# Bias rows at the gate projection, and attention by pairs of heads, in a one-core fp32 two-block kernel

## The chip, the cores and the metric

The kernel runs on one core of a Trainium2 chip. The metric is the device time of one execution in microseconds (us). A profiled execution gives, besides its time, a trace of every instruction and transfer; its span (first to last instruction) is a little shorter than its time.

## What is computed

Two transformer blocks in a row on x of 1 x 256 x 1024, all in fp32. The first has a hybrid mixer (a gated delta rule in chunks of 64, and a short convolution, joined by two sigmoid gates) and a SwiGLU FFN, both with adaptive norm. The second has causal attention with a relative bias by distance, 16 heads of 64, and a gated FFN with a convolution. With 256 positions the block selection of the attention leaves one block, so only the part of the query's own block counts:

```python
    s_own = jnp.einsum('bhqd,bhkd->bhqk', qi, k_own) * scale
    s_own = s_own + rel_bias[:, rel_bucket(qpos[:, None] - kpos_own[None, :])]
    s_own = jnp.where(kpos_own[None, :] <= qpos[:, None], s_own, NEG)
    ...
    p = jax.nn.softmax(jnp.concatenate(logits, axis=-1), axis=-1)
    out = jnp.einsum('bhqk,bhkd->bhqd', p[..., kk * BS:], v_own)
    ...
x = first_block(x, ...)          # mixer: w_in, gated delta rule, w_gdn_proj, w_o; FFN: w_ffn_in, w_ffn_out
y = rms_norm_2(h, attn_norm); qkv = y @ w_qkv; h = h + attention @ w_o_2
h = h + (silu(gate) * val) @ w_down   # gate, val = conv(rms_norm_2(h) @ w_up)
```

## The kernel before

All activations stay on the chip, feature-major (128 features of a tile on the partitions, 256 positions along the row). A weight comes in chunks of 1 MB (`raw`, four buffers), whose DMAs are issued on SP (lines 327 to 349). ACT copies a chunk's upper part (`whi`, rounded to the fast matmul format), and DVE or POOL makes the rest, `wlo = raw - whi` (`emit_event`, from line 368; `pool_free`, line 98, decides whether POOL gets a half chunk, 128x512, or DVE a full one, 128x1024). Every product is then three matmuls: `whi` by the high part of the activation, `whi` by its low part, `wlo` by the high part (the last loop of the quoted code). A unit is 128 output columns of one weight over all its rows.

The order of the instructions on each engine is set when the program is built. The main loop goes through the units in a fixed order and issues their matmuls; after each `k` it calls `tick`, which advances generators, one per piece of other work (`start(...)` puts one on the list): the delta rule's inversions and steps, the norms, the attention's heads. A generator's `yield` lets other work go first. How far each is advanced depends on a model of the engines' times, `et`, which `account` (line 111) keeps: it adds a cost for each instruction issued, and for a DMA one by its size, from the line that the change touches (line 118). All instructions are issued through one helper, so all have line 150 in the profile, and are told apart by the names of their tiles: `mm` and `sd` are PSUM tiles (main products and side products), `h1h`/`h1l`, `o`, `mixh`, `h2nh`, `ah`, `xah`, `oath` are activations in two parts, in the order of the stages: w_in (to about 340 us; its last piece is the projection of gate A), w_gdn_proj, w_o, FFN in, FFN out (from about 510 us), then w_qkv with the attention between its units (615 to 695), w_o_2, w_up, w_down.

The relative bias is kept as a table by distance. `rel_table` (line 1291) is started when the FFN's out projection begins (`rel_at`). It loads a one-hot matrix, multiplies the 16 x 32 bias by it (16 heads x 256 distances), writes the result behind NEG into `relr`, 16 partitions x 384, and sends that to DRAM 128 times per head in one DMA (`relscr`, 3,072 KB). Two gathers of 1 MB, `relb`, then read it with a row step of 383 instead of 384, so each partition gets the row shifted by one. These DMAs are on POOL's queue, as are the powers of the delta rule's output norm (`osc`).

The attention runs by heads. `att_probs(j, e)` makes the scores of head e of tile j (two heads of 64 share a tile of 128 features; each lies on one half of the partitions, so its matmuls use 64 rows): query positions 0 to 127 against keys 0 to 127, positions 128 to 255 against all keys. DVE adds the bias and takes the maximum, ACT exponentiates and sums, PE transposes three 128x128 blocks (`oats` into `oatp`). `att_out(j)` transposes the values, scales them, multiplies with the transposed probabilities as weights (six matmuls 128x64 a tile, three for each head), divides by the sums on DVE (`gx<-sd,rcp`), transposes the result back (two transposes of `gx`) and splits it into `oath` and `oatl`.

Of the kernel before, what the change touches and what calls it, by code (L numbers as in the profile page):

```python
# [11 lines left out]
F32 = mybir.dt.float32  # L12
F32R = mybir.dt.float32r
AF = mybir.ActivationFunctionType
# [58 lines left out]
def body(ctx, tc, a, out):  # L73
# [37 lines left out]
    def account(e, op, args, kw):  # L111
        if state["at"] is None:
            return
        n = size(args[0])
        late = dict(PE=0.2, V=0.25, A=0.42, G=0.15, SY=0.2)[e]
        if op == "dma_start":
            c, late = 1.0 if e == "G" else 0.06, 2.5
            st["dma"] = max(st["dma"], et[e], cur["dep"]) + size(args[0]) * P * MBUS
            late += max(0.0, st["dma"] - max(et[e], cur["dep"]))
        elif e == "PE":  # L120
            c = n / 2360.0 if args[1].dtype == F32R else max(n / 600.0, 0.213 if n == 1 else 0.107)
        elif e == "V":
# [1165 lines left out]

    relb = {}

    def rel_table():
        while not len(freeb):
            yield 0
        yield from space("gx")
# [27 lines left out]
    def post_qkv(kind, j):  # L1322
# [3 lines left out]
        def f(ps, rel):  # L1326
# [12 lines left out]
            else:  # L1339
# [2 lines left out]
                V.scalar_tensor_tensor(t, t, c_, rowa, op0=OP.add, op1=OP.mult)  # L1342
                done.add((kind, j))
                if kind == "k":
                    for e in range(2):
                        start(att_probs(j, e), 2)
                    start(att_out(j), 2)
            yield
        return f
# [9 lines left out]
    def att_probs(j, e):  # L1359
        att_alloc()  # L1360
        q, k = qkv["q"][:, j], qkv["k"][:, j]
        h = 2 * j + e
        r = slice(e * DH, (e + 1) * DH)
        while not len(room["P"]) or not len(freeb):
            yield 0
        pi = room["P"].popleft()
        p_ = oat["s"][:, 384 * pi:384 * pi + 384]
        i, b = bank()
# [3 lines left out]
        mx = wk.tile([P, 6], F32, name="mx", tag="mx", bufs=6)  # L1372
        if e == 0:
            pv[j] = wk.tile([P, 4], F32, name="rcp", tag="rcp", bufs=8)
        rc = pv[j]
        bt = relb[h // 8]
        V.tensor_tensor_reduce(p_[:, 0:P], b[:, 0:P], bt[:, h % 8, P:2 * P], scale=1.0, scalar=-3e38,
                               op0=OP.add, op1=OP.max, accum_out=mx[:, 0:1])
        V.tensor_tensor_reduce(p_[:, P:], b[:, P:3 * P], bt[:, h % 8, :], scale=1.0, scalar=-3e38,
                               op0=OP.add, op1=OP.max, accum_out=mx[:, 1:2])  # L1380
        freeb.append(i)
        V.tensor_scalar(mx[:, 2:4], mx[:, 0:2], -1.0, None, op0=OP.mult)
        yield 2
        A.activation(p_[:, 0:P], p_[:, 0:P], AF.Exp, bias=mx[:, 2:3], accum_out=mx[:, 4:5])
        A.activation(p_[:, P:], p_[:, P:], AF.Exp, bias=mx[:, 3:4], accum_out=mx[:, 5:6])
        yield 2
        V.reciprocal(rc[:, 2 * e:2 * e + 2], mx[:, 4:6])
        while not len(room["PT"]) or not len(freeb):
            yield 0
        ti = room["PT"].popleft()  # L1390
        i, b = bank()
        for m in range(3):
            PE.transpose(b[:, m * P:(m + 1) * P], p_[:, m * P:(m + 1) * P], ident)
        yield 1
        A.activation(oat["p"][:, ti], b[:, :384], AF.Copy)
        freeb.append(i)
        room["P"].append(pi)
        pv[j, e] = ti
        done.add(("pt", h))
        yield  # L1400

    def att_out(j):
# [13 lines left out]
        while any(("pt", 2 * j + e) not in done for e in range(2)):  # L1416
            yield 0
        yield 1
        yield from get()
        i, b = bank()  # L1420
        for e in range(2):
            pt = oat["p"][:, pv[j, e]]
            r = slice(e * DH, (e + 1) * DH)
# [7 lines left out]
        yield from space("gx")  # L1431
        yield 1
        yield from space("gx")
        o_t = take("gx")
# [3 lines left out]
        freeb.append(i)  # L1438
        yield 2
        yield from get()  # L1440
        i, b = bank()
        for t in range(2):
            PE.transpose(b[:, t * P:(t + 1) * P], o_t[:, t * P:(t + 1) * P], ident)
        give(o_t)
        yield 1
        A.activation(oat["h"][:, j], b[:, :S], AF.Copy)
        yield
# [144 lines left out]
    for jp in range(4):  # L1592
        pair_units(w_in, Q0, jp, post_q, h1)
        pair_units(w_in, GB0, jp, post_gb, h1)
        if jp % 2 == 0:
            sprinkle()
    for jp in range(4):
        pair_units(w_in, GA0, jp, post_ga, h1)
        if jp % 2 == 0:
            sprinkle()  # L1600
# [279 lines left out]
    for u, k0, k1, ahead in order:  # L1880
# [80 lines left out]
```

## Time and profile before

| | |
|---|---|
| times of three runs | 917.23, 912.41, 911.23 us |
| median | 912.41 us |
| the profiled execution | 916.82 us |
| its span | 915.0 us |
| mean granted clock of TensorE | 0.972 |
| busy: PE, DVE, ACT, POOL | 862.7, 697.1, 502.3, 154.0 us |
| bytes read and written in DRAM | 174.64 and 4.72 MB |

PE is TensorE's matmuls, DVE VectorE, ACT ScalarE, POOL GpSimd. A row of a group gives busy time, the mean of one instruction, and, behind the last bar, how long the engine was idle just before them and what ended most of that. A name such as `sd<-oats,oatp` is output, then inputs. q1 is the queue of the weights (SP), q0 that of POOL. Matmuls overlap, and their ends are modelled, so the start of the next one tells more than the end of one. Granted clock 1.00 is 2.4 GHz, 0.50 is 1.2.

### The profile page before, as it was taken

The numbers are of one execution on the slowest core, as the hardware profiler recorded it, in microseconds if no ns is written. First come the engines' busy times: TensorE is split into PE (matmuls) and PEld (weight loads), VectorE is DVE, ScalarE is ACT, GpSimd is POOL, SyncE is SP. The second block draws the span as 40 slices with busy tenths as digits, with TensorE's granted clock in tenths as the row PEclk, the third lists the DMA queues.
The fourth block names the chain that finished last, engine by engine and source line by source line (L and its number), as shares of the span: only waits on it lengthen the run. The fifth ranks groups of instructions, "written<-read, shape, count | busy, mean of one in ns | idle before, by whom it ended". The sixth has DMA issues, their size and how long they took to land.

```text
span 915.0 us, 17770 instructions
## 1 busy us (share of the span) xinstructions
PE 862.7 (94%) x7159; PEld 847.1 (93%) x7159; DVE 697.1 (76%) x1271; ACT 502.3 (55%) x904; POOL 154.0 (17%) x140
## 2 busy tenths in 40 slices
PE   6899999987899999999999996999999989999996
PEld 6889989986899999999999996998999989999995
DVE  5788998799867689979877534687666899888442
ACT  3328775453756755565454423567665566666341
POOL 3450023155110211232000001110002511000010
PEclk9879999998999999999999997999999999999998
DMA  9968595553914578667988699754243356555521
GB/s 292 282 186 275 185 291 172 161 181 116 315 58 138 184 231 283 227 227 261 337 279 280 182 111 323 257 185 138 93 139 106 126 195 222 189 191 171 185 71 46
DMA packets 164370, 180.51 MB, mean 197 GB/s; under 512 B 9052, under 2 KB 154832, under 8 KB 164288
## 3 DMA queue, kind: packets, MB, share of 16 engines
q1 hardware_dynamic: 161632, 172.57, 58.3%
q0 software_dynamic: 2144, 6.19, 4.1%
q8 instruction: 56, 0.92, 0.4%
q10 hardware_dynamic: 512, 0.62, 0.2%
q14 instruction: 26, 0.21, 0.1%
HBM read 174.64 MB, written 4.72 MB: 196 GB/s over the span
## 4 chain that ended last, share of the span: by engine, by line
PE 66%; DVE 14%; DMA 7%; issue 6%; ACT 4%; POOL 1%; SPq 0%; POOLq 0%; ACTq 0%; DVEq 0%
PE mm L150 56%; PE sd L150 10%; DVE wlo L150 4%; DMA raw<-in_w_ffn_out_dram 3%; DVE acc L150 2%; DVE ct L150 2%; ACT whi L150 2%; DMA raw<-in_w_in_dram 2%; DVE cv L150 2%; DVE KQ L150 1%; DMA xtok<-in_x_dram 1%; POOL wlo L150 1%; DMA KQ<-blk 1%; DMA raw<-in_w_gdn_proj_dram 1%; DVE ynt L150 1%
## 5 line engine op out<-in xcount | busy, mean ns | idle before, releaser
L150 DVE TENSOR_TENSOR wlo<-raw,whi 128x1024 fp32r<-128x1024 f32 (+1 forms) x244 | 293.8, 1211 | 95.4 <-ACT whi L150 95.0
L150 ACT ACTIVATE whi<-raw 128x1024 fp32r<-128x1024 f32 (+2 forms) x269 | 273.9, 1026 | 148.6 <-PE mm L150 102.1
L150 PE MATMUL mm<-h1h,whi 128*128 128x256 f32 x552 | 162.0, 296 | 0.6 <-ACT h1h L150 0.6
L150 PE MATMUL mm<-h1h,wlo 128*128 128x256 f32 x552 | 156.4, 285 | 4.2 <-DVE wlo L150 4.2
L150 PE MATMUL mm<-h1l,whi 128*128 128x256 f32 x552 | 156.3, 285 | 0.3
L150 PEld LDWEIGHTS mm<-h1h,wlo 128*128 128x128 f32 x552 | 106.4, 194 | 5.2 <-DVE wlo L150 5.0
L150 PEld LDWEIGHTS mm<-h1h,whi 128*128 128x128 f32 x552 | 106.8, 194 | 1.6 <-ACT h1h L150 1.0
L150 PEld LDWEIGHTS mm<-h1l,whi 128*128 128x128 f32 x552 | 106.7, 194 | 0.8 <-DVE h1l L150 0.7
L150 PE MATMUL mm<-ah,whi 128*128 128x256 f32 x352 | 100.6, 286 | 6.6 <-ACT whi L150 6.6
L150 POOL TENSOR_TENSOR wlo<-raw,whi 128x512 fp32r<-128x512 f32 (+1 forms) x41 | 66.0, 1630 | 242.0 <-ACT whi L150 229.3
L150 PE MATMUL mm<-ah,wlo 128*128 128x256 f32 x352 | 100.2, 285 | 0.5 <-DVE wlo L150 0.5
L150 PE MATMUL mm<-al,whi 128*128 128x256 f32 x352 | 100.0, 284 | 0.0
L150 DVE SCALAR_TENSOR_TENSOR acc<-raw,cact,acc 128x1024 f32<-128x1024 f32 (+1 forms) x78 | 85.5, 1096 | 1.9 <-DMA raw<-in_w_ada_f_dram 0.4
L150 PE MATMUL mm<-ynh,whi 128*128 128x256 f32 x288 | 81.6, 283 | 3.8 <-DVE gx L150 3.8
L150 PE MATMUL mm<-ynh,wlo 128*128 128x256 f32 x288 | 81.6, 283 | 0.0
L150 PE MATMUL mm<-ynl,whi 128*128 128x256 f32 x288 | 81.5, 283 | 0.0
L150 PE MATMUL mm<-h2nh,wlo 128*128 128x256 f32 x288 | 79.6, 276 | 1.3 <-DVE wlo L150 1.3
L150 PE MATMUL mm<-h2nh,whi 128*128 128x256 f32 x288 | 79.9, 278 | 0.5 <-DVE shc L150 0.5
L150 PE MATMUL mm<-h2nl,whi 128*128 128x256 f32 x288 | 79.5, 276 | 0.0
L150 PEld LDWEIGHTS mm<-ah,whi 128*128 128x128 f32 x352 | 68.8, 196 | 7.2 <-ACT whi L150 6.8
L150 PEld LDWEIGHTS mm<-ah,wlo 128*128 128x128 f32 x352 | 67.3, 191 | 0.8 <-DVE wlo L150 0.8
L150 PEld LDWEIGHTS mm<-al,whi 128*128 128x128 f32 x352 | 67.4, 192 | 0.0
(326 smaller groups left out, 2147.1 us busy)
## 6 DMA issues: line engine op xcount, KB each, us to landing
raw<-in_w_in_dram SPq DMA_DIRECT2D x30, 1024.0 KB, 5.9
raw<-in_w_ffn_in_dram SPq DMA_DIRECT2D x22, 1024.0 KB, 7.1
raw<-in_w_up_dram SPq DMA_DIRECT2D x22, 1024.0 KB, 5.1
raw<-in_w_ada_dram SPq DMA_DIRECT2D x16, 1024.0 KB, 5.4
raw<-in_w_qkv_dram SPq DMA_DIRECT2D x12, 1024.0 KB, 5.2
raw<-in_w_ada_dram SPq DMA_DIRECT2D x16, 512.0 KB, 6.6
raw<-in_w_o_dram SPq DMA_DIRECT2D x8, 1024.0 KB, 5.3
raw<-in_w_ada_f_dram SPq DMA_DIRECT2D x8, 1024.0 KB, 5.3
```

The costliest lines, as they stand in the source:

```text
L150: r = fn(*args, **kw)
```

## The change

It has three parts. The planner's cost of a DMA (line 118) is taken from all elements of the destination, where before a tile's first dimension was always counted as 128 partitions. The bias rows are computed by a generator of their own, `rel_rows`, started at the first unit of gate A's projection; it writes the 16 rows to DRAM (`relrow`, 24 KB) and repeats them with four DMAs from DRAM to DRAM, four heads each (768 KB); `rel_table`, at the old place, waits for these and issues only the two gathers. And the attention's `att_probs(j)` takes both heads of a tile, with their score matmuls in turn on the two row halves; the probabilities are divided by their sums before the transposes, by four DVE scalings a tile; `att_out` takes each head's values as weights (64 columns, so that the two heads' results lie on the two halves of the output partitions) and the transposed probabilities as the moving side, so that the output is feature-major at once, and the division and the two transposes behind it are gone.

```diff
-            st["dma"] = max(st["dma"], et[e], cur["dep"]) + size(args[0]) * P * MBUS
+            st["dma"] = max(st["dma"], et[e], cur["dep"]) + int(np.prod(args[0].shape)) * MBUS
...
-    def rel_table():
+    def rel_rows():
...
-        r = wk.tile([16, 384], F32, name="relr", tag="ot", bufs=1)
+        r = cst.tile([16, 384], F32, name="relr")
         V.memset(r, NEG)
         V.tensor_copy(r[:, :S], b[:16, :S])
         freeb.append(i)
-        sc = drp.tile([16, P, 384], F32, name="relscr")
-        G.dma_start(sc, r[:, None, :].to_broadcast([16, P, 384]))
+        row = drp.tile([16, 384], F32, name="relrow")
+        G.dma_start(row, r)
+        relb["s"] = drp.tile([16, P, 384], F32, name="relscr")
+        for h in range(0, NH, 4):
+            G.dma_start(relb["s"][h:h + 4], row[h:h + 4, None, :].to_broadcast([4, P, 384]))
+            yield 4
+        done.add("relrows")
+
+    def rel_table():
+        while "relrows" not in done:
+            yield 0
+        sc = relb["s"]
...
-        PE.matmul(b[:, 0:P], q[r, 0:P], k[r, 0:P], start=True, stop=True)
-        PE.matmul(b[:, P:3 * P], q[r, P:2 * P], k[r, :], start=True, stop=True)
+        for c0, n in ((0, P), (P, 2 * P)):
+            for e in range(2):
+                PE.matmul(b2[e][1][:, c0:c0 + n], q[r[e], c0:c0 + P], k[r[e], 0:n], start=True, stop=True)
+        et["PE"] -= (et["PE"] - t0) / 2
...
-        V.reciprocal(rc[:, 2 * e:2 * e + 2], mx[:, 4:6])
...
+        V.reciprocal(mx[:, :, 0:2], mx[:, :, 4:6])
+        for e in range(2):
+            V.tensor_scalar(p_[e][:, 0:P], p_[e][:, 0:P], mx[:, e, 0:1], None, op0=OP.mult)
+            V.tensor_scalar(p_[e][:, P:], p_[e][:, P:], mx[:, e, 1:2], None, op0=OP.mult)
...
-        for e in range(2):
-            pt = oat["p"][:, pv[j, e]]
-            r = slice(e * DH, (e + 1) * DH)
-            o0, o1 = (b[:, (2 * e + t) * DH:(2 * e + t + 1) * DH] for t in range(2))
-            PE.matmul(o0, pt[:, 0:P], vt[:, 0, r], start=True, stop=True)
-            PE.matmul(o1, pt[:, P:2 * P], vt[:, 0, r], start=True, stop=False)
-            PE.matmul(o1, pt[:, 2 * P:3 * P], vt[:, 1, r], start=False, stop=True)
+        for s_, c0 in ((0, 0), (1, P)):
+            for e in range(2):
+                r = slice(e * DH, (e + 1) * DH)
+                pt = oat["p"][:, pv[j, e]]
+                PE.matmul(b[r, c0:S], vt[:, s_, r], pt[:, s_ * S:s_ * S + S - c0], start=s_ == 0, stop=s_ == 1,
+                          skip_group_check=True)
...
-        V.tensor_tensor(o_t.rearrange("p (t e c) -> p e t c", e=2, c=DH),
-                        b[:, :S].rearrange("p (e t c) -> p e t c", e=2, c=DH),
-                        pv[j].rearrange("p (e t) -> p e t", e=2)[:, :, :, None].to_broadcast([P, 2, 2, DH]), OP.mult)
...
-        for t in range(2):
-            PE.transpose(b[:, t * P:(t + 1) * P], o_t[:, t * P:(t + 1) * P], ident)
...
+        if u["idx"] == rows_at:
+            start(rel_rows())
```

On POOL before, the bias's DMAs stand together in the FFN's stages, behind the norm's low parts (`h2nl`) and a last pair of splits:

```order
L150 TENSOR_TENSOR h2nl<-h2nt,h2nh 128x256 x8
L150 TENSOR_TENSOR wlo<-raw,whi 128x512 x2
L150 DMA gx_6202<-in_onehot_dram 32x256
L150 DMA relscr<-relr 2048x1x384
L150 DMA relb_6259<-relscr 128x8x256
L150 DMA relb_6261<-relscr 128x8x256
```

On POOL after, the one-hot matrix, the row and the four copies stand in gate A's projection and w_gdn_proj's, between the powers of the delta rule's last head group (`osc`):

```order
L150 DMA gx_3680<-in_onehot_dram 32x256
L150 DMA relrow<-relr 16x384
L150 DMA relscr<-relrow 512x1x384
L150 TENSOR_TENSOR osc<-ssq,nhalf 128x4
L150 DMA relscr<-relrow 512x1x384
L150 TENSOR_TENSOR osc<-osc,nhalf 128x4
L150 DMA relscr<-relrow 512x1x384 x2
L150 TENSOR_TENSOR wlo<-raw,whi 128x512 x2
```

The DMA from SBUF with 2,048 rows has become one of 16 rows and four of 512, and two `osc` powers stand behind the first and second copy; in the FFN's stages POOL now has the gathers alone behind the same splits:

```order
L150 TENSOR_TENSOR h2nl<-h2nt,h2nh 128x256 x8
L150 TENSOR_TENSOR wlo<-raw,whi 128x512 x2
L150 DMA relb_6212<-relscr 128x8x256
L150 DMA relb_6214<-relscr 128x8x256
```

No DMA stands before the two gathers there any more. On PE in the attention before (`mm` is w_qkv's projection, `qkvk,qkvq` the scores, `oats,oatp` the values' product):

```order
L150 MATMUL sd_7507<-qkvk,qkvq 128x128
L150 MATMUL sd_7507<-qkvk,qkvq 128x256
L150 MATMUL mm_7475<-xah,whi 128x258
L150 MATMUL mm_7475<-xal,whi 128x256
L150 MATMUL mm_7475<-xah,wlo 128x258
L150 MATMUL sd_7531<-qkvk,qkvq 128x128
L150 MATMUL sd_7531<-qkvk,qkvq 128x256
L150 MATMUL mm_7475<-xah,whi 128x258
L150 MATMUL mm_7475<-xal,whi 128x256
L150 MATMUL mm_7475<-xah,wlo 128x258
L150 MATMUL sd_7537<-oats,oatp 128x64 x6
L150 MATMUL sd_7544<-oats,oatp 128x64 x6
```

And on PE after, at the same place in the attention:

```order
L150 MATMUL sd_7537<-qkvk,qkvq 128x128
L150 MATMUL sd_7538<-qkvk,qkvq 128x128
L150 MATMUL sd_7537<-qkvk,qkvq 128x256
L150 MATMUL sd_7538<-qkvk,qkvq 128x256
L150 MATMUL mm_7490<-xah,whi 128x258
L150 MATMUL mm_7490<-xal,whi 128x256
L150 MATMUL mm_7490<-xah,wlo 128x258
L150 MATMUL mm_7490<-xah,whi 128x258
L150 MATMUL mm_7490<-xal,whi 128x256
L150 MATMUL mm_7490<-xah,wlo 128x258
L150 MATMUL sd_7550<-oatp,oats 64x256 x2
L150 MATMUL sd_7550<-oatp,oats 64x128 x2
```

The two heads' scores stand in turn in two PSUM tiles, and a tile's values take four matmuls into one, where each tile had six of 128x64.

## Rows read from the trace of the kernel before

**Rows 1.** the page, part 1: busy us, share of the span, instructions

```profile
PE 862.7 (94%) x7159; PEld 847.1 (93%) x7159; DVE 697.1 (76%) x1271; ACT 502.3 (55%) x904; POOL 154.0 (17%) x140
```

**Rows 2.** PE's waits in groups: us in total, times, longest us

```profile
PE sd L150 <- ACT gx L150: 10.3, 6, 5.8
PE mm L150 <- ACT whi L150: 6.6, 1, 6.6
```

**Rows 3.** table by stage: start:end, us, engines' busy (x), granted clock, DMA, GB/s

```profile
185.00:245.00 60.00, 47.29 (x371) 45.71 (x370) 57.58 (x86) 28.97 (x57) 28.77 (x19) 0.91 0.62 193
310.00:345.00 35.00, 35.00 (x307) 34.89 (x307) 28.26 (x41) 23.44 (x40) 3.91 (x3) 1.00 0.76 250
341.40:366.90 25.50, 24.35 (x213) 23.95 (x211) 25.14 (x40) 12.31 (x18) 3.05 (x2) 1.00 0.88 292
425.00:450.00 25.00, 25.00 (x223) 25.00 (x222) 23.67 (x29) 13.22 (x21) 0.00 (x0) 1.00 1.00 339
625.00:650.00 25.00, 24.72 (x202) 22.46 (x202) 17.98 (x90) 20.49 (x68) 0.00 (x0) 1.00 0.27 86
```

**Rows 4.** the same table, around the FFN's out projection

```profile
540.30:550.50 10.20, 10.20 (x88) 10.06 (x86) 3.21 (x8) 1.52 (x4) 0.00 (x0) 1.00 1.01 124
550.50:557.10 6.60, 0.07 (x1) 0.00 (x0) 0.00 (x0) 1.05 (x2) 2.54 (x3) 0.75 1.02 312
557.10:563.90 6.80, 6.28 (x27) 5.98 (x28) 6.11 (x6) 4.38 (x8) 1.79 (x2) 0.50 1.06 350
```

**Rows 5.** DMA 515 to 560 us; its last row: whole span

```profile
q0 software_dynamic: 808, 3.57, 64.8%
...
raw<-in_w_ffn_out_dram SPq DMA_DIRECT2D x4, 1024.0 KB, 31.3
relscr<-relr POOLq DMA_DIRECT2D x1, 3072.0 KB, 33.8
...
q1 hardware_dynamic: 161632, 172.57, 58.3%
```

**Rows 6.** POOL's timeline: start us, us, instruction

```profile
418.61 0.70 POOL L150 DMA_DIRECT2D gx<-in_onehot_dram  x1
```

**Rows 7.** DMA, 752 to 772 us: a queue, an issue with landing

```profile
q0 software_dynamic: 144, 0.52, 6.8%
...
fnw<-in_final_norm_dram POOLq DMA_DIRECT2D x1, 512.0 KB, 6.3
```

**Rows 8.** the chain of waits, 325 to 370: start us, us, what

```profile
335.79 5.17 DMA raw<-in_w_gdn_proj_dram
...
341.38 3.49 DVE wlo L150 x3
```

**Rows 9.** PE's timeline in the attention: start us, us, instruction

```profile
632.44 1.57 PE L150 MATMUL sd<-qkvk,qkvq 64*128 64x128 f32 x12
...
634.51 0.92 PE L150 MATMUL sd<-qkvk,qkvq 64*128 64x128 f32 x4
...
635.82 2.79 PE L150 MATMUL sd<-oats,oatp 128*128 128x64 f32 x24
638.42 0.36 PE L150 MATMUL mm<-xah,whi 128*128 128x258 f32 x1
...
638.85 1.15 PE L150 MATMUL sd<-cn,oats 128*128 128x128 f32 x9
639.76 0.36 PE L150 MATMUL mm<-xah,whi 128*128 128x258 f32 x1
...
643.83 0.93 PE L150 MATMUL sd<-qkvk,qkvq 64*128 64x128 f32 x8 [0.21 <-DVE qkvk L150]
644.69 0.39 PE L150 MATMUL mm<-xah,whi 128*128 128x258 f32 x1
```

**Rows 10.** PE's groups, 595 to 705: busy us, mean ns | idle

```profile
L150 PE MATMUL sd<-oats,oatp 128*128 128x64 f32 x96 | 11.5, 271 | 0.0
```

**Rows 11.** DVE's groups, 615 to 700, the same columns

```profile
L150 DVE TENSOR_TENSOR gx<-sd,rcp 128x256 f32<-128x256 f32 x8 | 3.4, 425 | 7.0 <-PE sd L150 6.9
```

More of the change, by code (lines that the diff above doesn't have):

```diff
@@ L1344, in f @@
                 if kind == "k":
-                    for e in range(2):
-                        start(att_probs(j, e), 2)
+                    start(att_probs(j), 2)
                     start(att_out(j), 2)
@@ L1357, in att_alloc, with att_probs @@
             room["P"], room["PT"], room["vt"] = Room(4), Room(8), Room(2)
-    def att_probs(j, e):
+    def att_probs(j):
         att_alloc()
         q, k = qkv["q"][:, j], qkv["k"][:, j]
-        h = 2 * j + e
-        r = slice(e * DH, (e + 1) * DH)
-        while not len(room["P"]) or not len(freeb):
+        while len(room["P"]) < 2 or len(freeb) < 2:
             yield 0
-        pi = room["P"].popleft()
-        p_ = oat["s"][:, 384 * pi:384 * pi + 384]
-        i, b = bank()
-        PE.matmul(b[:, 0:P], q[r, 0:P], k[r, 0:P], start=True, stop=True)
-        PE.matmul(b[:, P:3 * P], q[r, P:2 * P], k[r, :], start=True, stop=True)
-        yield 1
[L1372 to L1382, printed above, removed]
@@ new lines, in att_probs @@
+        r = [slice(e * DH, (e + 1) * DH) for e in range(2)]
+        pi = [room["P"].popleft() for e in range(2)]
+        p_ = [oat["s"][:, 384 * i:384 * i + 384] for i in pi]
+        b2 = [bank() for e in range(2)]
+        t0 = et["PE"]
+        for c0, n in ((0, P), (P, 2 * P)):
+            for e in range(2):
+                PE.matmul(b2[e][1][:, c0:c0 + n], q[r[e], c0:c0 + P], k[r[e], 0:n], start=True, stop=True)
+        et["PE"] -= (et["PE"] - t0) / 2
+        yield 1
+        mx = wk.tile([P, 2, 6], F32, name="mx", tag="mx", bufs=6)
@@ new lines, in att_probs @@
+        for e in range(2):
+            h, (i, b) = 2 * j + e, b2[e]
+            bt = relb[h // 8]
+            V.tensor_tensor_reduce(p_[e][:, 0:P], b[:, 0:P], bt[:, h % 8, P:2 * P], scale=1.0, scalar=-3e38,
+                                   op0=OP.add, op1=OP.max, accum_out=mx[:, e, 0:1])
+            V.tensor_tensor_reduce(p_[e][:, P:], b[:, P:3 * P], bt[:, h % 8, :], scale=1.0, scalar=-3e38,
+                                   op0=OP.add, op1=OP.max, accum_out=mx[:, e, 1:2])
+            freeb.append(i)
@@ L1383, in att_probs @@
+        V.tensor_scalar(mx[:, :, 2:4], mx[:, :, 0:2], -1.0, None, op0=OP.mult)
         yield 2
-        A.activation(p_[:, 0:P], p_[:, 0:P], AF.Exp, bias=mx[:, 2:3], accum_out=mx[:, 4:5])
-        A.activation(p_[:, P:], p_[:, P:], AF.Exp, bias=mx[:, 3:4], accum_out=mx[:, 5:6])
+        for e in range(2):
+            A.activation(p_[e][:, 0:P], p_[e][:, 0:P], AF.Exp, bias=mx[:, e, 2:3], accum_out=mx[:, e, 4:5])
+            A.activation(p_[e][:, P:], p_[e][:, P:], AF.Exp, bias=mx[:, e, 3:4], accum_out=mx[:, e, 5:6])
@@ L1386, in att_probs @@
         yield 2
-        V.reciprocal(rc[:, 2 * e:2 * e + 2], mx[:, 4:6])
[L1388 to L1393, printed above, removed]
-        yield 1
[L1395 to L1399, printed above, removed]
+        V.reciprocal(mx[:, :, 0:2], mx[:, :, 4:6])
@@ new lines, in att_probs @@
+        for e in range(2):
+            V.tensor_scalar(p_[e][:, 0:P], p_[e][:, 0:P], mx[:, e, 0:1], None, op0=OP.mult)
+            V.tensor_scalar(p_[e][:, P:], p_[e][:, P:], mx[:, e, 1:2], None, op0=OP.mult)
+        yield 1
+        for e in range(2):
+            while not len(room["PT"]) or not len(freeb):
+                yield 0
+            ti = room["PT"].popleft()
+            i, b = bank()
+            for m in range(3):
+                PE.transpose(b[:, m * P:(m + 1) * P], p_[e][:, m * P:(m + 1) * P], ident)
+            yield 1
+            A.activation(oat["p"][:, ti], b[:, :384], AF.Copy)
+            freeb.append(i)
+            room["P"].append(pi[e])
+            pv[j, e] = ti
@@ L1400, in att_probs @@
+        done.add(("pt", j))
         yield
@@ L1415, in att_out @@
         yield 1
-        while any(("pt", 2 * j + e) not in done for e in range(2)):
+        while ("pt", j) not in done:
             yield 0
@@ L1420, in att_out @@
         i, b = bank()
-        for e in range(2):
-            pt = oat["p"][:, pv[j, e]]
-            r = slice(e * DH, (e + 1) * DH)
-            o0, o1 = (b[:, (2 * e + t) * DH:(2 * e + t + 1) * DH] for t in range(2))
-            PE.matmul(o0, pt[:, 0:P], vt[:, 0, r], start=True, stop=True)
-            PE.matmul(o1, pt[:, P:2 * P], vt[:, 0, r], start=True, stop=False)
-            PE.matmul(o1, pt[:, 2 * P:3 * P], vt[:, 1, r], start=False, stop=True)
+        t0 = et["PE"]
+        for s_, c0 in ((0, 0), (1, P)):
+            for e in range(2):
+                r = slice(e * DH, (e + 1) * DH)
+                pt = oat["p"][:, pv[j, e]]
+                PE.matmul(b[r, c0:S], vt[:, s_, r], pt[:, s_ * S:s_ * S + S - c0], start=s_ == 0, stop=s_ == 1,
+                          skip_group_check=True)
+        et["PE"] -= (et["PE"] - t0) / 2
         for e in range(2):
@@ L1430, in att_out @@
         room["vt"].append(vi)
[L1431 to L1434, printed above, removed]
-        V.tensor_tensor(o_t.rearrange("p (t e c) -> p e t c", e=2, c=DH),
-                        b[:, :S].rearrange("p (e t c) -> p e t c", e=2, c=DH),
-                        pv[j].rearrange("p (e t) -> p e t", e=2)[:, :, :, None].to_broadcast([P, 2, 2, DH]), OP.mult)
[L1438 to L1441, printed above, removed]
-        for t in range(2):
-            PE.transpose(b[:, t * P:(t + 1) * P], o_t[:, t * P:(t + 1) * P], ident)
-        give(o_t)
         yield 1
@@ L1596, in body @@
             sprinkle()
+    rows_at = len(units)
     for jp in range(4):
```

## The prediction

> **What bounds the kernel now.** I read the page's busy times first: PE (TensorE) is busy for 862.7 us, 94% of the span [rows 1]. So two things can shorten the program: fewer or better packed matmuls, or the removal of one of PE's waits. Next come PE's waits, grouped by what ended them. Two groups bear on the edit's places: 6.6 us in one wait for a split weight (`whi`) and 10.3 us in six waits for `gx`, 5.8 of it in one [rows 2]. The table by stage says what stands behind PE in five stretches: 185 to 245 us has DVE full and PE idle for 12.7 of 60 us; from 310 to 345 PE never stops and DVE is idle for 6.7 us; from 341.4 to 366.9 DVE is full; from 425 to 450 the 16 DMA engines are full; in the attention, 625 to 650, PE is full, and neither DVE nor DMA is [rows 3].
>
> The longest single wait for a weight is at the start of the FFN's out projection. PE stands idle from 550.5 to 557.1, and then runs to 563.9 at a granted clock of 0.50, 1.2 of 2.4 GHz, with 27 matmuls where the stretch before it had 88 in 10.2 us [rows 4]. The transfers of that stretch name the cause: `relscr<-relr`, 3,072 KB, takes 33.8 us to land, and four weight chunks issued beside it take 31.3 us [rows 5] where one of the same size takes 5.17 in the gate stage [rows 8]; POOL's queue q0 moves 3.57 MB in 64.8% of 16 engines' time [rows 5]. That is 3.57 MB / (0.648 x 45 us x 16) = 7.7 GB/s per engine, where the weights' queue over the whole span has 172.57 MB / (0.583 x 915 x 16) = 20.2 [rows 5].
>
> **The change part by part.** Sums are made against the profiled execution, 916.82 us with a span of 915.0; it lies 4.4 above the median of 912.41.
>
> *The burst leaves the out projection.* What goes is the 6.6 us wait and the slow clock behind it. At 10.2/88 = 0.116 us a matmul the 27 of that stretch need 3.1 us and took 6.8, so 3.7 more: **-10.3 us**. Late next are the two gathers of 1 MB, which stay; more of them below.
>
> *Where the burst goes.* The same 3 MB are now written in the gate projection by four DRAM-to-DRAM copies of 768 KB. The trace has no such copy. The nearest transfer by kind is `fnw`, one DRAM row repeated over 128 partitions: 512 KB in 6.3 us, and its queue moved 0.52 MB in 6.8% of 20 us and 16 engines, 24 GB/s per engine [rows 7]. By that, 3.15 MB take 8.2 us of all engines. The upper bound is the old copy's 33.8 us, the lower nothing (the stage's DMA share is 0.76 [rows 3], so 35 x 0.24 = 8.4 us of engine time are free). I take a landing near 8 to 10 us and a cost of **+1**, because the stretch from 310 to 345 has 6.7 us of idle DVE to catch up with [rows 3].
>
> *A new wait on POOL.* The first copy reads `relrow`, so POOL's queue stands at it until the 24 KB row has landed: `fnw` on this queue lands in 6.3 us [rows 7], and I count some 5 for this smaller one. Behind it stand POOL's `osc` power and, behind that on DVE in order, the last head group's `osc`, then accumulations and weight splits. The chain shows how tight this is: a weight lands 5.17 us after 335.79, three splits follow at 341.38 [rows 8], and DVE is full from there on [rows 3]. Five us late on POOL shows at most as 5 us on PE, at least as 0 if the row is written before the power is wanted; most of it is taken up by the 6.7 us of slack: **+2** (0 to 6).
>
> *Gathers earlier.* The first gather can go where the one-hot DMA went, at 418.61 [rows 6], into a stretch whose DMA share is 1.00 [rows 3]. 1 MB at 20.2 x 16 GB/s is 3.2 us of the engines: **+1** (0 to 3).
>
> *Cost model of the planner.* The corrected size of a DMA moves instructions between 185 and 345 us. POOL loses 8 of its 128x512 splits, DVE gets them as 4 of 128x1024. DVE, which is full there (57.58 of 60 us [rows 3]), pays 4 x 3.49/3 = 4.7 us [rows 8]; POOL, 28.77 of 60 us busy, is rid of more than that, and what waited for its splits comes earlier. The stage's 12.7 us of idle PE can become less or more; nothing in a row decides it. I take **+1** (-6 to +5).
>
> *Attention, scores.* One head alone (four records) takes 0.92 us, two heads that stand together (eight) 0.93, three (twelve) 1.57 [rows 9]. The next matmul starts 0.86 us after the two heads (643.83 to 644.69), so 0.07 of each is a modelled end, and I take 0.85, 0.86 and 1.50: row halves already overlap where the order puts them side by side. In PE's timeline of before the 16 heads stand as five pairs, one group of three and three single heads, 4.3 + 1.5 + 2.6 = 8.4 us; now there are always pairs, 8 x 0.86 = 6.9: **-1.5**.
>
> *Attention, values.* The 128x64 matmuls go, 48 of them with two records each, 96 [rows 10]; 24 records, two tiles, take 638.42 - 635.82 = 2.60 us [rows 9], 1.30 a tile and 10.4 together. In place stand four matmuls a tile with 64 stationary columns each, two column halves with 256 and 128 moving columns. If the halves run side by side as the row halves do, a tile costs 0.86 like a pair of scores: 6.9, so -3.5. If not, it costs about the 1.50 of the group of three, in which only two heads overlap: 12.0, so +1.6. I take the first, since the column halves share neither weights' columns nor output partitions, as row halves share no rows; +1.6 stays the upper bound.
>
> The Trainium skill, TensorEngine Tiling (Array Packing), section Tiling Modes, states that tiles of the array load weights and multiply in parallel, and names column tiling for at most 64 stationary columns. The rows show it for row halves alone; no run of before has column halves. By the page the term would be the -3.5.
>
> *Attention, transposes and vector work.* 16 transposes of `gx` go; nine transposes take 639.76 - 638.85 = 0.91 us [rows 9], so 16 x 0.10 = **-1.6**. DVE loses 8 multiplications of 425 ns [rows 11] and gets 32 scalings of 128x128 and 128x256 at no more than 425 ns each, so at most 13.6 - 3.4 = 10.2 us more, over some 75 us in which it is idle for 7 of every 25 [rows 3]: nothing, as long as that idle time covers it, and all 10 us if it didn't. But the scaling stands between the exponential and the transposes, so a tile's transposes come later; PE has the next tiles' projections to put there, and I allow **+1** for new waits. Attention together: -1.5 - 3.5 - 1.6 + 1 = **-5.6** (-8 to 0).
>
> Sum: -10.3 + 1 + 2 + 1 + 1 - 5.6 = **-10.9**, so 905.9 for an execution like the profiled one, and 901.5 for the median.
>
> **The rivals.**
>
> *Column halves don't run side by side.* +1.6 in place of -3.5 gives 906.6. For it: no row shows two column halves at once. Against: row halves overlap fully [rows 9].
>
> *The copies hold the DMA engines in the gate stage (slower).* They write rows of 1,536 bytes to DRAM like the old copy, which ran at 7.7 GB/s per engine. If they too need T = 33.8 us, weights issued beside them land up to 31 us late. The stage can take about 12 us: 5.2 of a usual landing [rows 8] and 6.7 of idle DVE [rows 3]; after that DVE is full and nothing is won back. The loss is T - 12: 22 us in place of +1 and +2, so -10.9 - 3 + 22 = +8, 920.5; with a half-speed restart of PE of the kind in [rows 4] (3.7) 924. It decides from T = 12 + 10.9 + 3 = 26 us on, 3.15 MB at 121 GB/s. Against: `fnw` ran at three times the old copy's rate, so the slowness lies rather in the old copy's 16 source partitions, which the copies don't have.
>
> The Trainium skill, DMA: Bandwidth & Descriptors, section "Why a DMA increments its semaphore by 16 and not by 1", says that a transfer uses as many engines, at most 16, as divide the slowest dimension of both its sides. A copy's outer dimension is 4 heads, which would put each copy on four engines; were all on the same four, 3,072 KB at 20.2 GB/s each would be about 39 us, this rival's case; on different fours it would be 10. No row decides.
>
> *The stall isn't removed.* The second gather waits for PE's last read of the slot near 518 us, then competes with the same weight chunks. Against: 1 MB is a third of the burst. If the out projection still loses all 10.3: 911.8.
>
> *The order between 185 and 345 us decides.* The stage's 12.7 us of idle PE were some 5 us more or less: 906.5 or 896.5.
>
> **How the numbers follow.** The forecast holds 0.52, with a range of its own from 894 to 909. Serial column halves hold 0.20, the slow copies 0.10, a stall that stays 0.08, the order 0.10 in halves. A measurement of this kernel tells about 1% from no change, 903.3 and 921.5. Below 903.3 lie two thirds of the forecast (0.36), a third of the serial case (0.07), half of the order's case (0.05), and what falls below where an unknown term came out at its lower bound (0.07): 0.55. Slower by over 1% is the slow copies and their half-speed tail, with the unknown tails of the new POOL wait: 0.10. Between lies 0.35. The range runs from 889 (the attention at its lower bound, the order's gain and no cost on POOL: 901.5 - 2.4 - 5 - 2 - 1, rounded down by the spread of the runs) to 912 (the stall stays).
>
> **What would show it.** In the profile after: no PE wait for `whi` over 2 us near 550, and no stretch at clock 0.50 behind it; weight chunks of `w_ffn_out` that land in 5 to 8 us; four `relscr` copies with landings of 8 to 12 us between 310 and 345 and PE without a gap over 1 us up to 367; `relb` issued near 418; score pairs and value groups that each take about 0.9 us; PE busy some 10 us less than 862.7 (6.6 in the attention, 3.7 from the clock). Wrong would be: copies that land in over 25 us, chunks of `w_gdn_proj` beside them that land in over 15, PE waiting for `wlo` between 340 and 370; value groups of 1.5 us; PE waiting for `oats` in the attention; or another sum of PE's idle time between 185 and 245 than 12.7.

## The result and the profile after

| | before | after |
|---|---|---|
| median of the runs | 912.41 us (11 runs) | 905.53 us (11 runs) |
| lowest and highest | 907.89, 917.23 | 900.14, 911.60 |
| profiled execution, its span | 916.82, 915.0 | 904.03, 902.3 |
| ratio of the runs | | 0.9917, 95% interval 0.9892 to 0.9942 |

The change makes the kernel 0.83% faster, 5.3 to 9.9 us by the interval. That lies inside the range, 4.0 us above the forecast of 901.5, and in the band "within 1%", which had a chance of 0.35; the likelier band, faster by more than 1% (0.55), did not come. The two profiled executions are 12.8 us apart, because that of before lies 4.4 us above its median and that of after 1.5 below.

PE's busy time in the page after answers to [rows 1]; then come the longest of PE's waits, in groups (us in total, times, longest us), which answer to [rows 2]:

```profile
PE 852.0 (94%) x7111; PEld 833.1 (92%) x7111; DVE 703.4 (78%) x1283; ACT 497.3 (55%) x900; POOL 144.1 (16%) x136
```

```profile
PE sd L150 <- DVE acc L150: 11.7, 5, 5.0
PE sd L150 <- ACT gx L150: 9.4, 5, 5.5
```

PE is busy for 10.7 us less. The wait for `whi` of 6.6 us has gone from the list, and the waits for `acc` now head it with a longest of 5.0 us; before, the three waits of that group made 6.1 us, the longest 2.8. The transfers around the FFN's out projection after (queues; issues with the median us to landing) answer to [rows 5]:

```profile
q0 software_dynamic: 272, 1.05, 6.9%
...
raw<-in_w_ffn_out_dram SPq DMA_DIRECT2D x4, 1024.0 KB, 5.2
...
relb<-relscr POOLq DMA_DIRECT2D x1, 1024.0 KB, 7.7
```

The weights land in 5.2 us instead of 31.3, and POOL's queue takes 6.9% of the engines instead of 64.8%. The cost has turned up in w_gdn_proj's stage. The table by stage, before and then after (start:end, us, busy of PE, PEld, DVE, ACT, POOL, granted clock, DMA share, GB/s):

```profile
322.00:346.00 24.00, 24.00 (x214) 24.00 (x213) 20.58 (x29) 12.87 (x25) 2.92 (x2) 1.00 0.80 261
```

```profile
322.00:346.00 24.00, 19.05 (x163) 18.88 (x162) 15.15 (x20) 9.13 (x21) 6.55 (x6) 0.96 1.01 323
...
344.58:347.70 3.12, 3.12 (x15) 3.12 (x16) 1.69 (x2) 0.00 (x0) 0.00 (x0) 0.51 1.11 325
```

In the same 24 us PE worked without a pause before; after, it lacks 5 us, the DMA share has gone from 0.80 to 1.01, and PE comes back at a granted clock of 0.51, 1.2 of 2.4 GHz, behind 4.95 us of idle time. The transfers of that stretch after show who fills the engines:

```profile
q1 hardware_dynamic: 3048, 4.57, 58.9%
q0 software_dynamic: 2813, 3.17, 42.1%
...
relscr<-relrow POOLq DMA_DIRECT2D x4, 768.0 KB, 16.9
raw<-in_w_gdn_proj_dram SPq DMA_DIRECT2D x3, 1024.0 KB, 15.6
raw<-in_w_ada_dram SPq DMA_DIRECT2D x2, 1024.0 KB, 12.4
```

3.17 MB in 42.1% of 24 us and 16 engines is 19.6 GB/s per engine: the copies run as fast as the weights (20.2, [rows 5]), so they need 10 us of all 16 engines, and they need them together with six chunks of weights. The 16.9 us are for one copy of 768 KB; from the issue of the first (322.08) to the landing of the last (346.85) the four together take 24.8. The chain of waits shows one of the chunks, 13.80 us where [rows 8] has 5.17:

```profile
334.17 13.80 DMA raw<-in_w_gdn_proj_dram
```

And PE's timeline and DVE's after show what PE ran into: the transposes of an adaptive-norm chunk whose accumulation (`acc`) came late, because its chunk of `w_ada`, issued at 329.39, took 12.4 us to land. In PE's order these transposes stand six matmuls into w_gdn_proj:

```profile
339.36 0.28 PE L150 MATMUL mm<-o,wlo 128*128 128x256 f32 x1
344.58 1.09 PE L150 MATMUL sd<-cn,acc 128*128 128x128 f32 x4 [4.95 <-DVE acc L150]
```

```profile
341.83 2.60 DVE L150 SCALAR_TENSOR_TENSOR acc<-raw,cact,acc 128x1024 f32<-128x1024 f32 x2 [1.60 <-DMA raw<-in_w_ada_dram]
```

The attention came out as forecast. PE's timeline after (pairs of scores `qkvk,qkvq`, value groups `oatp,oats`) and its groups, which answer to [rows 9, 10], and DVE's new scalings, beside [rows 11]:

```profile
641.06 0.87 PE L150 MATMUL sd<-oatp,oats 128*64 128x256 f32 x8
641.86 0.39 PE L150 MATMUL mm<-xah,whi 128*128 128x258 f32 x1
...
642.42 0.93 PE L150 MATMUL sd<-qkvk,qkvq 64*128 64x128 f32 x8
643.27 0.39 PE L150 MATMUL mm<-xah,whi 128*128 128x258 f32 x1
```

```profile
L150 PE MATMUL sd<-oatp,oats 128*64 128x256 f32 x32 | 5.2, 405 | 0.0
...
L150 PE MATMUL sd<-oatp,oats 128*64 128x128 f32 x32 | 3.1, 273 | 0.0
```

```profile
L150 DVE TENSOR_SCALAR oats<-oats,mx 128x256 f32<-128x256 f32 x16 | 5.6, 348 | 0.0
...
L150 DVE TENSOR_SCALAR oats<-oats,mx 128x128 f32<-128x128 f32 x16 | 4.5, 284 | 0.3
```

A value group takes 0.80 us to the start of the next matmul, a pair of scores 0.85. The scalings take 10.1 us on DVE, the eight multiplications of before (3.4 [rows 11]) are gone, and PE waits once for the probabilities, 0.7 us.

### The profile page after: what moved, and what is told of

Read it like the earlier page. It is cut to its first block, busy times and chain, and to the rows that moved or that the text cites. A ratio compares the mean times of both kernels' runs of the same rounds, so it can differ in the third digit from the quotient of the medians.

```text
span 902.3 us, 17691 instructions
## 1 busy us (share of the span) xinstructions
PE 852.0 (94%) x7111; PEld 833.1 (92%) x7111; DVE 703.4 (78%) x1283; ACT 497.3 (55%) x900; POOL 144.1 (16%) x136
## 4 chain that ended last, share of the span: by engine, by line
PE 57%; DVE 22%; issue 7%; DMA 6%; ACT 6%; POOL 1%; SPq 1%; POOLq 0%; ACTq 0%; DVEq 0%
PE mm L150 48%; PE sd L150 9%; DVE wlo L150 6%; DVE acc L150 4%; DVE cv L150 3%; ACT whi L150 3%; DVE ct L150 2%; DVE KQ L150 2%; DMA raw<-in_w_gdn_proj_dram 2%; DMA raw<-in_w_ffn_in_dram 1%; DMA raw<-in_w_in_dram 1%; DMA raw<-in_w_ada_dram 1%; DVE AK L150 1%; ACT L150 1%; DMA KQ<-blk 1%
## 5 line engine op out<-in xcount | busy, mean ns | idle before, releaser
L150 DVE TENSOR_TENSOR wlo<-raw,whi 128x1024 fp32r<-128x1024 f32 (+1 forms) x248 | 298.4, 1209 | 88.8 <-ACT whi L150 88.7
L150 PE MATMUL mm<-ah,whi 128*128 128x256 f32 x352 | 97.9, 278 | 0.0
L150 PE MATMUL mm<-ah,wlo 128*128 128x256 f32 x352 | 97.7, 277 | 0.0
L150 PE MATMUL mm<-al,whi 128*128 128x256 f32 x352 | 97.7, 277 | 0.0
L150 POOL TENSOR_TENSOR wlo<-raw,whi 128x512 fp32r<-128x512 f32 (+1 forms) x33 | 55.2, 1697 | 234.5 <-ACT whi L150 234.5
L150 PEld LDWEIGHTS mm<-ah,whi 128*128 128x128 f32 x352 | 66.1, 188 | 0.0
```

Of the source, the lines that this page charges most:

```text
L150: r = fn(*args, **kw)
```

## The experiments

To compare executions I cut each span at the first matmul of a stage in PE's timeline ("the rest" begins at w_up); the stages, in us. The kernels are named by the words in brackets below; `after_again` is the changed kernel once more:

```
kernel       to w_gdn_proj  w_gdn_proj   w_o   FFN in  FFN out  qkv+att.  w_o_2  the rest
before            340.14      22.68    23.46  126.81   73.13    99.73    24.56   204.52
acct_only         340.55      22.68    24.21  126.82   72.49    99.73    24.56   199.84
attn_only         342.53      22.68    24.24  129.52   71.83    94.07    24.76   201.11
no_attn           342.40      28.25    24.21  128.46   62.19    99.76    24.56   201.06
after             338.79      29.26    23.53  127.63   59.84    94.02    24.76   204.41
after_again       340.33      31.41    23.89  127.84   59.84    94.03    24.76   199.98
late_copies       339.43      25.28    23.47  127.74   59.84    94.07    24.76   199.71
one_copy          340.89      31.93    23.46  127.67   59.84    94.05    24.76   199.47
twice             340.68      29.66    30.65  127.56   59.84    94.09    24.76   199.94
rows_q1           338.61      22.68    23.47  127.64   59.84    94.07    24.76   203.76
by_head           341.78      22.68    23.47  127.83   59.84    94.11    24.77   198.84
tiny              341.94      22.68    24.20  127.90   59.84    94.03    24.76   199.92
```

The theory after the result: the copies take DMA engines from the weights of w_gdn_proj's stage, so that stage loses 6 to 9 us of what the out projection wins. The rivals: POOL's wait for the 24 KB row holds up `osc` and what hangs on it; the planner's new order does it; or the four copies load the engines unevenly.

**The parts alone.** Three kernels take parts of the change: the kernel before with the planner's line alone (acct_only, the diff), the kernel before with the new `att_probs` and `att_out` alone (attn_only), and the kernel after with the old `att_probs` and `att_out` (no_attn).

```diff
-            st["dma"] = max(st["dma"], et[e], cur["dep"]) + size(args[0]) * P * MBUS
+            st["dma"] = max(st["dma"], et[e], cur["dep"]) + int(np.prod(args[0].shape)) * MBUS
```

Expected of the planner's line alone:

> The kernel before with the planner's DMA cost alone. If the change's wait at the first ada transposes of the w_gdn_proj stage (4.95 us near 344 in the changed kernel) comes from the new order, it stands here too, and this kernel is 4 to 7 us slower than before. If the copies make it, this kernel has no wait over 1 us between 320 and 365, keeps the 6.6 us stall of the FFN's out projection, and is within 3 us of before.

Measured: 911.92 us, ratio 0.9972 (0.9951 to 0.9993). The stage of w_gdn_proj stays at 22.68 us, and the stall is there, in PE's waits from 320 to 600 us:

```profile
PE mm L150 <- ACT whi L150: 7.0, 1, 7.0
```

So the new order alone doesn't make the wait near 344. By the ratio it gains 0.6 to 4.5 us, but the trace doesn't show where: the stages up to w_o_2 differ by +0.5 us together, and the 4.7 us of the last column are about what two executions of one and the same kernel differ by there (204.41 and 199.98, after and after_again).

Expected of the attention alone:

> The kernel before with the attention's edit alone. Column halves that run side by side: -5.6 us from the first scores to w_o_2's first matmul, as in the changed kernel, and a value group of 0.9 us. Column halves one after the other: -0.5 us and value groups of 1.5. The stall of the FFN's out projection stays in both.

Measured: 908.17 us, ratio 0.9938 (0.9912 to 0.9965), and in its trace the stretch from w_qkv to w_o_2 shrinks from 99.73 to 94.07, -5.66 us. The one wait of PE in it, from 625 to 700 us:

```profile
PE sd L150 <- DVE oats L150: 0.7, 1, 0.7
```

Expected of the rest without the attention:

> The changed kernel with the old attention (planner's cost and bias rows stay). If the parts add up, it is the changed kernel plus 5.6 us, 911 of a median, about 2 us under before: the out projection's 10.3 us are won and some 6 to 7 lost between 340 and 365. If the attention's gain was an artefact of the pair of profiled executions, it is as fast as the changed kernel.

Measured: 910.11 us, ratio 0.995 (0.9921 to 0.9978). w_gdn_proj takes 28.25 us and FFN out 62.19: 5.6 lost, 10.3 won against the 72.49 of the planner's line alone. Within their intervals the parts add up: -0.50% and -0.62% against -0.83% and, in a second set of runs of the changed kernel, -0.94%.

**The copies earlier** (rows_q1). The bias rows start at the second pair of the q and gate B projections, where little is transferred.

```diff
     for jp in range(4):
+        if jp == 1:
+            rows_at = len(units)
         pair_units(w_in, Q0, jp, post_q, h1)
         pair_units(w_in, GB0, jp, post_gb, h1)
...
-    rows_at = len(units)
```

> The changed kernel with the bias rows started 12 units earlier, at the second pair of the q and gate B projections, where the changed kernel's DMA share is 0.07 to 0.28 (250 to 280 us). If the copies' share of the DMA engines makes the wait at 344, that wait goes, w_gdn_proj's chunks land in 5 to 8 us instead of 15.6, and the kernel is 5 to 7 us faster than the changed one (about 899). If POOL's wait for the row or the order makes it, the wait stays at 3 us or more, and the gain is under 2.

Measured: 895.13 us, ratio 0.9798 (0.9763 to 0.9834), 1.19% or 10.9 us under the changed kernel's ratio, more than the 5 to 7 expected. The stage of w_gdn_proj gives 6.6 of these; the two traces differ by 7.4 in all, and where the other executions gain more isn't shown. PE's timeline and DVE's show the same pair as above, now in time:

```profile
339.63 0.60 PE L150 MATMUL sd<-cn,acc 128*128 128x128 f32 x4
```

```profile
335.87 2.60 DVE L150 SCALAR_TENSOR_TENSOR acc<-raw,cact,acc 128x1024 f32<-128x1024 f32 x2
```

PE comes to these transposes at 339.63, just where it stood in the kernel after (339.36 and the last matmul). `acc` ends at 338.47, 1.16 us ahead; after, it ends at 344.43, 5.96 us later: 5.96 - 1.16 = 4.8 us late, the wait of 4.95. The chunks of w_gdn_proj land in 7.5 us from 310 to 350 and those of w_ada, on which `acc` waits, in 5.4 instead of 12.4, as the first two rows below say. The copies themselves are little faster where they are now (the next two rows, 250 to 280 us), though the weights' queue fills only 19.3% of the engines there; a weight chunk beside them needs 14.4 us there too, but PE has no wait in that stretch (last row, 255 to 280):

```profile
raw<-in_w_gdn_proj_dram SPq DMA_DIRECT2D x4, 1024.0 KB, 7.5
raw<-in_w_ada_dram SPq DMA_DIRECT2D x3, 1024.0 KB, 5.4
```

```profile
relscr<-relrow POOLq DMA_DIRECT2D x4, 768.0 KB, 14.9
raw<-in_w_in_dram SPq DMA_DIRECT2D x1, 1024.0 KB, 14.4
```

```profile
255.00:280.00 25.00, 25.00 (x221) 23.54 (x219) 13.80 (x28) 15.79 (x36) 7.29 (x7) 1.00 0.54 171
```

This version is faster than the kernel before and the changed one.

**The row early, the copies late** (late_copies). POOL no longer has a landing to wait for.

```diff
...
+        relb["row"] = row
+        yield
+
+    def rel_copies():
+        row = relb["row"]
         for h in range(0, NH, 4):
             G.dma_start(relb["s"][h:h + 4], row[h:h + 4, None, :].to_broadcast([4, P, 384]))
             yield 4
         done.add("relrows")
...
```

> The changed kernel with the row (one-hot matmul and the 24 KB DMA) made early, at the second pair of the q and gate B projections, and only the four copies left at gate A's projection. POOL then waits for no landing between 300 and 330 us. If POOL's wait for the row delayed the work, the wait of PE near 344 falls under 2 us and the kernel is about 5 us faster than the changed one. If the copies' transfers do it, a wait of 3 to 6 us stays there, w_gdn_proj's chunks land in 12 us or more, and the time is the changed kernel's within 2 us.

Measured: 899.58 us, ratio 0.9847 (0.9809 to 0.9886), and a wait between the two expectations:

```profile
343.03 0.63 PE L150 MATMUL sd<-cn,acc 128*128 128x128 f32 x4 [2.42 <-DVE acc L150]
```

This run did not tell the two apart: the time, 6.4 us under the changed kernel's by the ratio, fits the first expectation, the 12.3 us in which w_gdn_proj's chunks land fit the second. Without the row's landing ahead of them two of the four copies were issued from 310.16 on, 12 us earlier than in the changed kernel, so the bytes moved too. What was needed was a kernel with the wait and without the bytes.

**The wait without the bytes** (tiny). The kernel with the early rows, and at gate A's projection the same chain once more, with 6 KB behind the wait instead of 768. The additional work has no part in the output.

```diff
...
+        if not real:
+            sm = drp.tile([16, 384], F32, name="reltiny")
+            for h in range(0, NH, 4):
+                G.dma_start(sm[h:h + 4], row[h:h + 4])
+                yield 4
+            return
...
+        if u["idx"] == small_at:
+            start(rel_rows(False))
```

> The kernel with the early rows, and at gate A's projection the same chain once more with nothing behind it: one-hot matmul, a 24 KB row to DRAM, and four DMAs that wait for it on POOL as the copies did, of 6 KB each. This is the wait on POOL without the bytes. If the wait costs the 2 us (0 to 6) of the prediction, the stretch from the first w_gdn_proj matmul to the first w_o matmul grows from 22.7 us to over 24 and a wait stands near 344. If only the bytes cost, that stretch stays at 22.7 within 0.5, and the time is that of the kernel with the early rows.

Measured: 894.39 us, ratio 0.9786 (0.9746 to 0.9825); w_gdn_proj at 22.68 us to the hundredth, and no wait of PE between 320 and 365. POOL did wait, and `osc` did stand behind it, as its timeline shows:

```profile
325.13 0.50 POOL L150 DMA_DIRECT2D reltiny<-relsmall  x1 [3.53 <-DMA relsmall<-relq]
325.65 1.04 POOL L150 TENSOR_TENSOR osc<-ssq,nhalf 128x4 f32<-128x4 f32 x1
```

So the wait on POOL costs nothing here, and the loss belongs to the bytes.

**One copy instead of four** (one_copy). The trace of the change made an uneven spread possible: of the first copy's 16 completions in the trace after twelve come by 330.1 us and the last four at 336.8 to 338.5. That agrees with the Trainium skill, DMA: Bandwidth & Descriptors, section "Why a DMA increments its semaphore by 16 and not by 1", by which an outer dimension of 4 puts a copy on four engines.

```diff
-        for h in range(0, NH, 4):
-            G.dma_start(relb["s"][h:h + 4], row[h:h + 4, None, :].to_broadcast([4, P, 384]))
-            yield 4
+        G.dma_start(relb["s"], row[:, None, :].to_broadcast([NH, P, 384]))
+        yield 4
```

> The changed kernel with the same 3,072 KB in one DMA over all 16 heads instead of four over 4 heads. If the bytes alone delay the weights, they still need some 10 us of all 16 engines, the copy lands in about 10 to 17 us, and PE's wait near 344 stays at 3 us or more. If it is the uneven spread of the four copies over the engines (four late completions of sixteen in each), the one copy lands in under 12 us, and the wait falls under 2 us.

Measured: 903.55 us, ratio 0.9911 (0.9881 to 0.9941), the changed kernel's time. The landing of the one copy is 19.8 us (24.8 for the four together), and PE's wait is longer than with four:

```profile
relscr<-relrow POOLq DMA_DIRECT2D x1, 3072.0 KB, 19.8
```

```profile
348.44 1.09 PE L150 MATMUL sd<-cn,acc 128*128 128x128 f32 x4 [6.71 <-DVE acc L150]
```

The spread is not the cause. The trace of the kernel after would have said so: the expectation has four late completions in each copy, but only the first has four; the second, third and fourth have 8, 12 and 16 (339.9 to 341.4, 342.3 to 343.9, 344.2 to 346.9 us). That fits a set of four engines of its own for each copy, so that the four together load all 16 once.

**The copies twice** (twice).

```diff
-        for h in range(0, NH, 4):
+        for h in range(0, 2 * NH, 4):
+            h = h % NH
```

> The changed kernel with each of the four copies issued twice, the same bytes to the same place, so 6 MB instead of 3. If their share of the DMA engines makes the wait, 10 us more of engine time in a stage whose DMA share is 1.03 make PE's waits between 340 and 370 longer by 6 to 12 us. If it is POOL's order or the planner's, they grow by under 2.

Measured: 909.2 us, ratio 0.9968 (0.9945 to 0.9991). The expectation missed the place: between 340 and 370 PE waits once, 4.4 us, no longer than in the changed kernel. The second set waited on POOL for the landing of the first, was issued from 341.4 on, and hit w_o's chunks (322 to 375 us), one of which took 18.4 us to land; PE waits 4.3 us (1.2 after) for `mixh` and `mixl`, whose work stands on DVE and ACT behind the splits of these chunks, between 372 and 379. w_gdn_proj and w_o together take 60.3 us where the changed kernel has 52.8, +7.5:

```profile
relscr<-relrow POOLq DMA_DIRECT2D x8, 768.0 KB, 17.1
...
raw<-in_w_o_dram SPq DMA_DIRECT2D x4, 1024.0 KB, 13.6
```

Three more megabytes cost 7.5 us by these stages, as three cost 6 to 9, one stage later.

**Head by head** (by_head). The scores' and values' matmuls of a tile, first one head's, then the other's.

```diff
-        for c0, n in ((0, P), (P, 2 * P)):
-            for e in range(2):
+        for e in range(2):
+            for c0, n in ((0, P), (P, 2 * P)):
                 PE.matmul(b2[e][1][:, c0:c0 + n], q[r[e], c0:c0 + P], k[r[e], 0:n], start=True, stop=True)
...
-        for s_, c0 in ((0, 0), (1, P)):
-            for e in range(2):
+        for e in range(2):
+            for s_, c0 in ((0, 0), (1, P)):
```

> The kernel with the early rows, with the scores and the values' matmuls written head by head (both of one head, then both of the other) instead of in turn. If standing next to each other is enough for the halves to overlap, as the pairs of the kernel before suggest, a pair of scores stays at 0.93 us and a value group at 0.87. If they overlap only in turn, values become 1.2 to 1.5 us and the attention 2 to 5 us longer.

Measured: 893.87 us, ratio 0.979 (0.9752 to 0.9829), and the same groups in PE's timeline:

```profile
637.66 0.88 PE L150 MATMUL sd<-oatp,oats 128*64 128x256 f32 x8
...
639.02 0.93 PE L150 MATMUL sd<-qkvk,qkvq 64*128 64x128 f32 x8
```

The turn within a tile is worth nothing. The single records of this value group show that the halves overlap all the same: they start in pairs 13 to 14 ns apart, the first two at 637.660 and 637.673 (6 to 7 ns in the kernel after, 641.063 and 641.070), and the next pair 0.25 us later. Standing next to each other is enough, and that the change gives to all eight tiles.

**The changed kernel again** (after_again).

> The changed kernel once more, unaltered, on the chip of the run before it: the wait near 344 comes again with 4 to 6 us and clock 0.50 behind it, and the stretch from the first w_up to the end of w_down, in which the program does not differ, shows whether single executions differ by some 5 us (139.6 and 134.9 us in executions so far).

Measured: 905.16 us, ratio 0.9906 (0.9869 to 0.9942), with a wait of 5.32 us at 346, a granted clock of 0.5 behind it, and w_gdn_proj at 31.41 us. The rest of the program from w_o_2 on differs by 4.4 us between two executions of one and the same kernel; the section on the hardware below has the rows.

## Why the prediction was right, and where it was wrong

The direction and the range held. The sum held in part by luck, because errors of opposite sign met in it. By its terms:

- *The stall of the out projection, -10.3.* Right, and a little small. The kernels with the old burst take 73.13, 72.49 and 71.83 us for FFN out, those without it 59.84, or 62.19 in one case: -10 to -13. The wait and the half-speed restart are as they were computed; up to 2.3 us more come from a slower pace of the matmuls, which I hadn't read (below).
- *The copies, +1.* This is the step that failed. The prediction took "a landing near 8 to 10 us", at `fnw`'s rate, and let "6.7 us of idle DVE" cover it. The rate was nearly right: 19.6 GB/s per engine against 24. But a landing was not bytes by rate over all 16 engines: one copy took 16.9 us, the four 24.8, and the weights beside them 12.4 and 15.6. The company of the weights is only part of it, since at the early place, with few weights, a copy still took 14.9 us; no run separates the parts. The free share of 0.24 was a mean over 35 us, and even that left 8.4 us of engine time for what measured 10. The cover was wrong too: PE's next need was not a weight split by DVE but the transposes of an adaptive-norm chunk, which in rows_q1, without the copies there, were ready only 1.16 us ahead. The term measured +5.6 to +8.7 (28.25, 29.26 and 31.41 less 22.68), with the slow clock behind the wait in it.
- *The new wait on POOL, +2.* It was there (3.25 us in the trace after, 3.53 in the kernel without the bytes) and costs nothing: 22.68 us with it and without.
- *Gathers earlier, +1.* Measured by the stage FFN in: 126.81 before, 127.63 after, +0.8. That can't be put down to the gathers: attn_only, which has them where before has them, takes 129.52. The first gather is issued at 423.91, 5.3 us behind 418.61, as is the stage.
- *The planner's line, +1.* Between -0.6 and -4.5 by its own runs, inside the bounds of -6 to +5. PE's idle time between 185 and 245 us is 10.0 us in acct_only and 10.9 after, where before has 12.7; but w_gdn_proj starts at 340.55 in acct_only and at 340.14 before, so that this gain isn't kept, and the trace names no other.
- *Attention, -5.6.* Measured -5.7 in both pairs of kernels that differ in nothing else. Value groups at 0.80 instead of 0.86, scores as computed, one new wait of 0.7 where I had allowed 1.

With the measured terms: -10.3 to -13.3, +6.6, 0, +0.8, -2.5 and -5.7 make -11 to -14 for the pair of profiled executions (-12.8). The medians, which don't share before's high execution, make -7.6 by the ratio; the other executions have no trace, so where they differ from the profiled ones stays open. The two wrong terms together, +6.6 and 0 in place of +1 and +2, turn the forecast of 901.5 into 905.1, next to the measured 905.53; that closeness is luck in part, since other terms are off by up to 3 us.

*The rivals.* Serial column halves: refuted, 0.87 us by record for a value group. A stall that stays: refuted by the kernels without the burst. The order: small, w_gdn_proj starts 1.35 us earlier after than before. The slow copies were the right place and the right mechanism, at a third of the size: +6.6 where that rival had +22. Its T is the time of all 3.15 MB, 24.8 us here, and its rule, T - 12, would give 12.8; it fails because the 12 us of cover were not what covered. The prediction gave this rival an all-or-nothing T of 33.8 us and no middle.

*The signs.* Of the signs of being wrong three came: chunks of `w_gdn_proj` over 15 us (15.6), a wait for `oats` (0.7 us, once), and another sum of idle time between 185 and 245. PE's wait in w_gdn_proj's stage was for `acc`, which no sign names. In the chances, two thirds of 0.52 are 0.35 and not 0.36, which changes nothing.

The Trainium skill's rule on array packing (TensorEngine Tiling (Array Packing), section Tiling Modes) agrees with the trace for column halves as well: the two heads' records start 6 to 7 ns apart, and a group takes 0.80 us for two halves of 64 columns, where the six 128x64 matmuls of before took 1.30.

## What to carry to other kernels

A burst that is moved keeps its bytes: price it as bytes over the engines' rate against the free engine time of the very microseconds in which it will run, and ask which transfer PE needs first there, and by how much it is early. Then look in the DMA row of the profile for a stretch where the share is low and PE has work: issuing the same 3 MB 64 us earlier was worth 1.2% of the kernel by the medians, of which 6.6 us (0.7%) are traced to their cause. A wait on an engine's queue (POOL's 3.5 us here) need not cost anything: ask what stands behind it and when PE wants that.

## What the runs showed of the hardware

*The copy from 16 SBUF partitions was slow, the same bytes from DRAM were not.* The old copy's records have 672 packets of 4,608 bytes at a mean of 658 ns; the new copies' records, again 672 of that size, are at 193 ns. Same bytes, same destination, both in company of weights: 33.8 us to land against 19.8 for the one copy of 3,072 KB and 24.8 for the four together. Whether it is the 16 partitions or SBUF as the source, no run here separates.

*A full-speed matmul has two paces.* At a granted clock of 0.99 to 1.00 consecutive 128x256 matmuls of one and the same kernel start either 0.113 or 0.118 us apart, over long stretches. Here is the larger part of w_up and w_down in two executions of the changed kernel, the table by stage of after and of after_again:

```profile
734.00:862.50 128.50, 128.50 (x1082) 128.50 (x1082) 101.62 (x162) 78.22 (x119) 3.20 (x4) 0.99 0.57 187
```

```profile
738.00:861.40 123.40, 123.40 (x1079) 123.40 (x1078) 101.92 (x162) 78.30 (x119) 3.14 (x4) 0.99 0.60 195
```

As many matmuls but for three records, the same clock, PE never idle, and 5.1 us apart. In the out projection before the pace went from 0.113 to 0.118 at the one-hot matmul of the bias, near 517.6 us, and stayed there to the stage's end; without that matmul it was 0.113 throughout (59.84 us for 528 matmuls), but for one kernel with 0.118 (62.19). What sets it stays open, and no run was made on it. A pair of profiled executions can differ by 5 us from this alone, so terms are to be read from stages and totals from medians.
